# Keeping the split parts of a decoder's weights in DRAM between token quarters

## The chip, the cores and the metric

The kernel runs on one core of a Trainium2 chip. The metric is the device time of one execution in microseconds (us); lower is better. Three runs of the kernel before took 2722.57 to 2724.44 us, median 2723.67.

## The reference

One layer of a decoder trunk for 2048 tokens of 1024 channels, all in float32. Three groups of heads (GLA, HGRN2, mLSTM) mix the tokens chunk by chunk; one output projection and a squared-ReLU feed-forward follow. Cut to what matters here:

```python
h = modulated_rmsnorm(x, norm_mix[l], shift1, scale1)
z = h @ w_in[l]                       # 1024 -> 4,5k columns
mixed = concatenate([gla_group(...), hgrn2_group(...), mlstm_group(...)])
x = x + gate1 * (mixed @ w_out[l])    # 1024 x 1024
h = modulated_rmsnorm(x, norm_mlp[l], shift2, scale2)
x = x + gate2 * (square(relu(h @ w_ff1[l])) @ w_ff2[l])   # 1024 -> 4096 -> 1024
out = rms(x) * final_norm
```

## The kernel before, in words

The 2048 tokens are four quarters of 512 (`NQ`, `TQ`). First comes the input projection of all quarters (`inproj`), its results stored to DRAM. Then, quarter by quarter, the output projection (`outproj`) and the feed-forward, whose 32 hidden tiles go in six blocks (`f1` makes a hidden tile, `f2` adds a block's share to the accumulator `acc`). The token mixing (`block_pass`, `chunk`, `chunk_out`) is emitted in small steps between the dense products by `pump`, at a pace set by due times; the mixing of quarter q + 1 runs beside the feed-forward of quarter q and is done ahead of its last block, where `outproj` of quarter q + 1 stands too.

Dense products run in the format fp32r, which keeps fewer bits than float32. To hold float32's precision every operand is split in two parts, the rounded value (hi) and the rest (lo), and each product is three passes over the parts (`PASSES`). `split` (lines 175 to 177) makes them: a cast on ACT (L176) and a subtraction on DVE (L177).

Weights come in pieces of [128, 1024] float32, 512 KB. `weights` (line 179) loads a piece into a raw buffer (tag `raw`, two of them, SP's queue, L184) and splits it into a buffer `wt` of [128, 2, 1024], 1 MB (tag `wt`, three of them, four in the pool `lp` of the last quarter's last block). A quarter uses 8 pieces of w_out, 32 of w_ff1 and 32 of w_ff2, and every quarter loads and splits them anew: 288 loads. A piece serves 24 products of 128 x 512 (three passes of eight tiles).

A scheduler puts each engine's instructions in order when the program is built, by priorities that follow the order of the code, which `ahead()` raises by 60 instructions and `late()` lowers by 20, and by when buffers come free. On the chip each engine and each queue then works strictly in that order. SP's queue holds the weight loads, the stores of x1 (L930) and of the output (L1004), and the loads of x; POOL's queue holds the mixing's loads and stores and the loads of `acc`.

The last quarter's output projection is drawn ahead: it runs after the fourth block of the third quarter's feed-forward, with its operands in `lp`.

Of the kernel before, what the change touches and what calls it, by code (L numbers as in the profile page):

```python
# [6 lines left out]
F32 = mybir.dt.float32  # L7
F32R = mybir.dt.float32r
# [6 lines left out]
P = 128  # L15
# [5 lines left out]
EPS = 1e-6  # L21
# [80 lines left out]
def trunk(ctx, tc, I, out):  # L102
    nc = tc.nc
    V, A, G, T = nc.vector, nc.scalar, nc.gpsimd, nc.tensor
    dma = nc.sync.dma_start
# [44 lines left out]
    def ahead():  # L150
        """What the dense products wait for goes before the token mixing in each engine's order."""
        return tc.high_priority(offset=lead[0])
# [4 lines left out]
    def late():  # L157
        """Products of the token mixing give way to so many instructions that came after them."""
        return tc.high_priority(offset=-LATE)

# [8 lines left out]
    def ln_exp(after):  # L169
        """The set with Exp and Ln, behind the activation after; what the caller adds to the stack runs behind it."""  # L170
        with tc.issue_after(after.ins):
            p_ = A.preload_act_table_set("natural_log_exp_and_others")
        return tc.issue_after(p_.ins)
# [5 lines left out]
    def weights(src, n, lp=None):  # L179
        """A [128, n] piece of weights as its two parts, [128, 2, n]."""  # L180
        with ahead():
            raw = wp.tile([P, 1024], F32, tag="raw", name="raw", bufs=2)
            r = raw[:, 0:n]
            dma(out=r, in_=src)  # L184
            wt = (lp or wp).tile([P, 2, 1024], F32R, tag="wt", name="wt", bufs=4 if lp else 3)
            split(wt[:, 0, 0:n], wt[:, 1, 0:n], r)
        return wt[:, :, 0:n]
# [10 lines left out]
    def modulate(hi, lo, src, rs, a_, b_, tmp=None):  # L198
        """hi + lo = src * a_ * rs + b_; the product goes to src's place if there is no tmp."""
        tmp = src if tmp is None else tmp  # L200
        V.scalar_tensor_tensor(out=tmp, in0=src, scalar=a_, in1=rs, op0=ALU.mult, op1=ALU.mult)
        A.activation(out=hi, in_=tmp, func=AF.Identity, bias=b_)  # L202
        V.scalar_tensor_tensor(out=lo, in0=tmp, scalar=b_, in1=hi.bitcast(F32), op0=ALU.add, op1=ALU.subtract)

    def sq_acc(sm, src, first, over=False):
        """Adds src ** 2 (to be kept in src's place if over) and its share of EPS to sm."""
        if first:
            return A.activation(out=sm, in_=src, func=AF.Square)
        sq = src if over else m5()[:, 0:src.shape[-1]]
        last = A.activation(out=sq, in_=src, func=AF.Square)  # L210
        V.scalar_tensor_tensor(out=sm, in0=sm, scalar=EPS / 7 * KT, in1=sq, op0=ALU.add, op1=ALU.add)
        return last

    def newton(x, y, t, scale):
        """One step of y towards (x * scale + EPS) ** -0.5; x and t are overwritten."""
        V.tensor_scalar(out=x, in0=x, scalar1=scale, scalar2=EPS, op0=ALU.mult, op1=ALU.add)
        V.tensor_tensor(out=t, in0=y, in1=y, op=ALU.mult)
        V.scalar_tensor_tensor(out=t, in0=t, scalar=-0.5, in1=x, op0=ALU.mult, op1=ALU.mult)
        V.scalar_tensor_tensor(out=y, in0=t, scalar=1.5, in1=y, op0=ALU.add, op1=ALU.mult)
# [12 lines left out]
    # ---------------------------------------------------------------- conditioning  # L232
    ada_tags, acc_tags = [], ["prod", "sdt", "alb"]

    def ada(m, o, n, slow=False):
        """Channels o .. o + n of modulation vector m; slow: in steps and beside the rest, in the buffers of those."""
# [39 lines left out]
    # ---------------------------------------------------------------- token mixing  # L276
# [16 lines left out]
    def block_pass(q, s):  # L293
        """Scores of tokens at most 15 apart within blocks of 16 tokens, for 48 channels per group."""
# [27 lines left out]
    def gates(q):  # L322
        """mLSTM gate rows of a quarter (row 32 n + h: chunk n, head h): running stabiliser and what follows."""
# [77 lines left out]
    def chunk(q, n, L, N):  # L401
        """Up to the normalised outputs of chunk n; N is the next chunk of the quarter."""
        nxt = (lambda f: f(q, n + 1, N)) if N else (lambda f: None)
        pt = lambda nm: psm.tile([P, 512], F32, tag="psm", name=nm)
        # channel-major q, k, f
# [66 lines left out]
        # mLSTM scores  # L472
# [24 lines left out]
        # diagonal blocks of the gated groups' scores  # L497
# [9 lines left out]
        # mLSTM output  # L507
# [37 lines left out]
        # scores of the gated groups  # L545
# [71 lines left out]
        # norms, output gates  # L617
# [36 lines left out]
    def both(a, b):  # L654
        """The steps of two independent generators by turns."""
        its = [a, b]
        while its:
            for g in list(its):
                try:
                    yield next(g)  # L660
                except StopIteration:
                    its.remove(g)
# [14 lines left out]
    # ---------------------------------------------------------------- input projection  # L677
# [34 lines left out]
    def h_stats_slow(q, res):  # L712
        """The same for quarter q in steps, its loads a step ahead."""
        sm = stat("sm", 2)
        x = []
        for k in range(0, KT + 2, 2):
            x += [load_x(q, i) for i in range(k, min(k + 2, KT))]
            for i in range(max(k - 2, 0), k):
                last = sq_acc(sm, x[i], i == 0, True)
            yield  # L720
        rs = stat("rs", 1)
        rstd(rs, sm, last)
        res.append(rs)
# [6 lines left out]
    def inproj(q, hts, nxt):  # L730
# [62 lines left out]
        def part(g, c0, n, ps, kk):  # L793
            """Two k-tiles' share of n columns of a group (of n // 128 channel tiles of the convolution)."""
# [76 lines left out]
    # ---------------------------------------------------------------- output projection and feed-forward  # L871
    R.x1 = [dp.tile([P, KT, TQ], F32, name=f"x1{q}") for q in range(NQ)]

    def spare(spec, src):
        """Eight [128, 512] tiles in buffers that the chunks leave free, loaded from src."""
        ts = []
        for tag, n, bufs in spec:
            t = m1.tile([P, n, TQ], F32, tag=tag, name="spare", bufs=bufs)
            ts += [t[:, i, :] for i in range(n)]
        for k, t in enumerate(ts):  # L880
            dma_m(out=t, in_=src(k))
        return ts
# [23 lines left out]
    def outproj(q, mt, lp=None):  # L906
# [9 lines left out]
        for dt in range(KT):  # L916
            xr = xs[dt] if xs else load_x(q, dt)
            w = weights(I["wo"][dt].rearrange("p c n -> p (c n)"), 1024)
# [14 lines left out]
    def ffn_in(h2, q, xs, sm, last, lp=None):  # L933
        """The feed-forward's input into the list h2, in steps."""
# [16 lines left out]
    def f1(h2, ft):  # L951
        w = weights(I["w1"][ft].rearrange("p c n -> p (c n)"), 1024)
# [15 lines left out]
    def w2_part(b, i, lp=None):  # L968
        return weights(I["w2"][F0[b] + i].rearrange("p u n -> p (u n)"), 1024, lp)

    def f2_tile(hds, b, acc, w, dt, c):
        """Block b's share of channel tile dt for the tokens c of a quarter; w: from the number of a part to the part."""
# [33 lines left out]
    def final_steps(q, acc):  # L1006
        """The final norm of a quarter, in steps."""
        sm = stat("sm", 2)
        for dt in range(KT):
            last = sq_acc(sm, acc[:, dt, :], dt == 0)  # L1010
            if dt % 4 == 3:
                yield
        rs = stat("rs", 1)
        rstd(rs, sm, last)
        yield
        final(q, acc, rs)
        yield

    def f2_last(lp, hds, acc):
        """The last block and the final norm by halves of the tokens, the first norm beside the second half's products."""  # L1020
# [16 lines left out]
    # ---------------------------------------------------------------- schedule  # L1037
# [26 lines left out]
    def step():  # L1064
        """One step of the block passes (which run ahead) or of the chunks."""
# [10 lines left out]
    def pump(us):  # L1076
        """Token mixing beside us of dense products, at the pace that the nearest deadlines ask for."""
# [112 lines left out]
# How the emission of the token mixing is paced beside the dense products, in us of the tensor engine's dense work  # L1190
# where the comment gives no other unit.
SLACK = (20, 60, 60, 60)    # by which a quarter's mixing is to be done before it is due
LAST = 1480                 # when the last quarter's mixing is due
FILL = 20.0                 # mixing emitted behind the first quarter's output projection
LOAD = 5.0                  # from a block pass's loads to its arithmetic
RUN = 0.2                   # share of the next quarter's block passes that goes beside a quarter's chunks
AHEAD = 60                  # instructions by which weights and evacuations go before the mixing
LATE = 20                   # instructions by which the mixing's products give way
STATS = 14                  # step of the input projection at which the next quarter's norm starts
BG = (24, 12, 20)           # steps of the input projection beside which the other modulation vectors are made  # L1200
EARLY = 3                   # feed-forward block of the last but one quarter behind which the last one's x1 is made
# [19 lines left out]
```

## Time and profile before

| | us |
|---|---|
| median of three runs | 2723.67 |
| span of the profiled execution (first to last instruction) | 2721.9 |
| PE busy | 2636.9 (97%) |
| DVE busy | 1792.1 (66%) |
| ACT busy | 1231.6 (45%) |
| HBM read, written | 336.21 MB, 62.95 MB |

The profiled execution's own time is its span and what lies around it; the median of the runs is 1.8 us above that span. PE is TensorE's products, PEld its weight loads, DVE VectorE, ACT ScalarE, POOL GpSimd, SP the queue of SyncE. A row `ps_f<-ht,wt` names what an instruction writes and reads; `raw<-w` is a load of a feed-forward piece, `raw<-wo` one of w_out. "DMA share" is the mean busy share of the core's 16 DMA engines. Windows are in us from the start of the span.

By time: input projections to 842 us, output projection of the first quarter from 844, its feed-forward from 900, the second quarter's output projection from 1317, the third's from 1805, the fourth's from 2236, and dense products alone after that.

### The profile page before, as it was taken

How to read it: one execution, taken by the hardware profiler on the slowest of the kernel's cores; microseconds unless marked ns; L12 is line 12 of the kernel's file. 1: busy time of each engine (PE TensorE's matmuls, PEld its weight loads, DVE VectorE, ACT ScalarE, POOL GpSimd, SP SyncE). 2: the span in 40 equal slices, each digit the busy share in tenths (PEclk: the TensorE clock that was granted, in tenths of full speed). 3: DMA queues.
4: the chain of work that ended last, by engine and by line, in shares of the span. 5: the costliest groups of instructions: out<-in, count | busy, mean ns of one | idle time of the engine just before them, and what ended most of it. 6: DMA issues, size and time to landing. Idle time of an engine off the chain costs nothing.

```text
span 2721.9 us, 39555 instructions
## 1 busy us (share of the span) xinstructions
PE 2636.9 (97%) x15050; PEld 2212.7 (81%) x15050; DVE 1792.1 (66%) x3345; ACT 1231.6 (45%) x2190; POOL 259.2 (10%) x434
## 2 busy tenths in 40 slices
PE   6999999999999999999999999999999999999998
PEld 5888898898888777788877888788877788888887
DVE  8785687977776877776887655457556556533335
ACT  4654445445543543454453445345445543433333
POOL 0101110020201102112110000100000000000000
PEclk9999999999999999999999999999999999999999
DMA  8776675585547424445454333344433245342332
GB/s 259 222 227 185 176 238 167 174 231 176 160 140 217 116 82 135 126 133 165 132 177 125 118 120 113 117 140 146 145 119 111 89 129 176 107 146 93 95 99 78
DMA packets 160200, 401.76 MB, mean 148 GB/s; under 512 B 20473, under 2 KB 60490, under 8 KB 160010
## 3 DMA queue, kind: packets, MB, share of 16 engines
q1 hardware_dynamic: 129338, 306.51, 35.7%
q0 software_dynamic: 30672, 92.73, 12.4%
q8 instruction: 118, 1.93, 0.3%
q14 instruction: 72, 0.59, 0.1%
HBM read 336.21 MB, written 62.95 MB: 147 GB/s over the span
## 4 chain that ended last, share of the span: by engine, by line
PE 50%; DVE 2%; ACT 1%; DMA 1%; issue 0%; DVEq 0%; ACTq 0%; SPq 0%
PE ps_f L155 40%; PE ps_op L155 5%; PE ps_a L163 2%; DVE wt L177 1%; DMA raw<-w 1%; PE ps_oh L163 1%; PE ps_og L163 1%; PE ps_t L167 0%; PE ps_x L167 0%; DVE acc L1000 0%; PE ps_mv L163 0%; ACT wt L176 0%; PE ps_uh L163 0%; PE ps_ug L163 0%; PE ps_ms L155 0%
## 5 line engine op out<-in xcount | busy, mean ns | idle before, releaser
L155 PE MATMUL ps_f<-ht,wt 128*128 128x512 f32 (+1 forms) x5472 | 1307.9, 393 | 4.8 <-ACT ht L202 4.8
L155 PEld LDWEIGHTS ps_f<-ht,wt 128*128 128x128 f32 x5472 | 1003.9, 189 | 213.4 <-ACT ht L202 5.0
L177 DVE TENSOR_TENSOR wt<-raw,wt 128x1024 fp32r<-128x1024 f32 (+3 forms) x436 | 498.8, 1145 | 412.8 <-ACT wt L176 411.7
L176 ACT CAST wt<-raw 128x1024 fp32r<-128x1024 f32 (+3 forms) x436 | 431.4, 990 | 640.1 <-PE ps_f L155 345.3
L155 PE MATMUL ps_ip<-wt,ht 128*128 128x384 f32 (+2 forms) x3072 | 604.5, 353 | 32.9 <-ACT st L782 8.7
L155 PEld LDWEIGHTS ps_ip<-wt,ht 128*128 128x128 f32 x3072 | 550.4, 191 | 61.1 <-ACT st L782 10.3
L982 DVE SCALAR_TENSOR_TENSOR acc<-ps_f,mod,acc 128x512 f32<-128x512 f32 (+1 forms) x200 | 145.2, 727 | 129.2 <-PE ps_f L155 128.4
L962 ACT ACTIVATE m<-ps_f 128x512 f32<-128x512 f32 x128 | 76.7, 599 | 318.5 <-PE ps_f L155 318.2
L155 PE MATMUL ps_f<-h,wt 128*128 128x512 f32 x768 | 181.4, 397 | 0.0
L155 PEld LDWEIGHTS ps_f<-h,wt 128*128 128x128 f32 x768 | 144.6, 188 | 35.6 <-issue 0.5
L155 PE MATMUL ps_op<-ht,wt 128*128 128x512 f32 x576 | 133.1, 393 | 5.7 <-ACT ht L176 3.8
L155 PEld LDWEIGHTS ps_op<-ht,wt 128*128 128x128 f32 x576 | 108.8, 190 | 29.2 <-ACT ht L176 3.9
L301 POOL DMA_DIRECT2D blk<-zq x144 | 93.6, 663 | 344.1 <-DVE prod L311 204.2
L567 DVE TENSOR_TENSOR td<-ps_a,td 128x384 f32<-128x384 f32 (+2 forms) x96 | 40.6, 423 | 110.8 <-PE ps_a L163 110.3
L311 DVE TENSOR_TENSOR prod<-blk 128x768 f32<-128x768 f32 (+3 forms) x192 | 111.2, 579 | 2.9
L312 DVE TENSOR_REDUCE Sd<-prod 128x48 f32<-128x768 f32 (+3 forms) x192 | 110.5, 575 | 3.0
L965 DVE TENSOR_TENSOR ht<-m,ht 128x512 fp32r<-128x512 f32 x128 | 88.1, 688 | 22.8 <-ACT m L964 22.3
L310 DVE TENSOR_TENSOR blk<-blk 128x720 f32<-128x720 f32 (+4 forms) x180 | 98.9, 549 | 0.0
L155 PE MATMUL ps_ip<-ht,wt 128*128 128x512 f32 x384 | 98.4, 404 | 0.0
L155 PEld LDWEIGHTS ps_ip<-ht,wt 128*128 128x128 f32 x384 | 71.4, 191 | 14.9 <-issue 0.7
L964 ACT ACTIVATE m<-m 128x512 f32<-128x512 f32 x128 | 81.0, 633 | 2.6
L963 ACT ACTIVATE ht<-m 128x512 fp32r<-128x512 f32 x128 | 81.1, 634 | 0.1
(393 smaller groups left out, 2627.2 us busy)
## 6 DMA issues: line engine op xcount, KB each, us to landing
raw<-w SPq DMA_DIRECT2D x256, 512.0 KB, 3.5
raw<-wg SPq DMA_DIRECT2D x100, 384.0 KB, 3.8
m<-wada SPq DMA_DIRECT2D x64, 256.0 KB, 3.7
raw<-wo SPq DMA_DIRECT2D x32, 512.0 KB, 3.5
m<-xq SPq DMA_DIRECT2D x56, 256.0 KB, 3.3
raw<-wg SPq DMA_DIRECT2D x28, 512.0 KB, 4.4
blk<-zq POOLq DMA_DIRECT2D x144, 96.0 KB, 6.1
zt<-zq POOLq DMA_DIRECT2D x48, 288.0 KB, 3.9
```

The lines of the kernel that those rows point to most:

```text
L155: T.matmul(out=ps, lhsT=l, rhs=r, start=start, stop=stop)
L163: T.matmul(out=ps, lhsT=l, rhs=r, start=start, stop=stop)
L176: A.copy(out=hi, in_=src)
L177: V.tensor_tensor(out=lo, in0=src, in1=hi.bitcast(F32), op=ALU.subtract)
L301: dma_m(out=t[i][32 * g:32 * g + 32], in_=src)
L310: V.tensor_tensor(out=t[1][:, 0:n, :], in0=t[1][:, 0:n, :], in1=t[2][:, d:16, :], op=ALU.mult)
L311: V.tensor_tensor(out=prod[:, 0:n, :], in0=t[1][:, 0:n, :], in1=t[0][:, d:16, :], op=ALU.mult)
L312: V.tensor_reduce(out=s49[:, 0:n, d:d + 33:16], in_=prod[:, 0:n, :].rearrange("p j (u c) -> p j u c", c=16), op=ALU.add, axis=AX.X)
L963: A.activation(out=hd[:, 0], in_=r, func=AF.Square)
L964: A.activation(out=r, in_=r, func=AF.Square)
L965: V.tensor_tensor(out=hd[:, 1], in0=r, in1=hd[:, 0].bitcast(F32), op=ALU.subtract)
L982: V.scalar_tensor_tensor(out=acc[:, dt, c], in0=ps, scalar=mod[:, 40 + dt:41 + dt], in1=acc[:, dt, c], op0=ALU.mult, op1=ALU.add)
```

## The change

The first use of each piece of w_out, w_ff1 and w_ff2 stays a load and a split, and the two parts are then stored to a DRAM tile of their own (`kept`). Each later use of the same piece loads both parts, 1 MB, from there straight into `wt`, with no raw buffer and no split. The store of a piece is held back by one piece (`save(1)`: at most one stays unsaved when the next raw load is issued), and all that are left are stored ahead of a load from `kept` (`save(0)`). The keys are the matrix and the number of the piece. `weights` takes its `wt` buffer ahead of the raw buffer now. The pieces of the input projection have no key and are treated as before. The change also drops docstrings and comments, so line numbers shift by up to 17.

```diff
+    kept, unsaved = {}, []
+
+    def save(left):
+        while len(unsaved) > left:
+            dst, wt = unsaved.pop(0)
+            dma(out=dst, in_=wt.bitcast(F32))
+
-    def weights(src, n, lp=None):
+    def weights(src, n, lp=None, key=None):
         with ahead():
+            wt = (lp or wp).tile([P, 2, 1024], F32R, tag="wt", name="wt", bufs=4 if lp else 3)
+            if key in kept:
+                save(0)
+                dma(out=wt.bitcast(F32), in_=kept[key])
+                return wt
+            save(1 if key else 0)
             raw = wp.tile([P, 1024], F32, tag="raw", name="raw", bufs=2)
             r = raw[:, 0:n]
             dma(out=r, in_=src)
-            wt = (lp or wp).tile([P, 2, 1024], F32R, tag="wt", name="wt", bufs=4 if lp else 3)
             split(wt[:, 0, 0:n], wt[:, 1, 0:n], r)
+            if key:
+                kept[key] = dp.tile([P, 2, 1024], F32, name="parts_%s%d" % key)
+                unsaved.append((kept[key], wt))
         return wt[:, :, 0:n]
...
-            w = weights(I["wo"][dt].rearrange("p c n -> p (c n)"), 1024)
+            w = weights(I["wo"][dt].rearrange("p c n -> p (c n)"), 1024, None, ("o", dt))
...
-        w = weights(I["w1"][ft].rearrange("p c n -> p (c n)"), 1024)
+        w = weights(I["w1"][ft].rearrange("p c n -> p (c n)"), 1024, None, ("a", ft))
...
-        return weights(I["w2"][F0[b] + i].rearrange("p u n -> p (u n)"), 1024, lp)
+        return weights(I["w2"][F0[b] + i].rearrange("p u n -> p (u n)"), 1024, lp, ("b", F0[b] + i))
```

What that makes of the order, at three places. SP's queue at the passage from the first quarter's output projection to its feed-forward, before:

```order
L184 DMA raw<-wo 128x1024
L913 DMA acc<-xq 128x512 x8
L184 DMA raw<-wo 128x1024 x3
L184 DMA raw<-w 128x1024 x60
L184 DMA raw<-wo 128x1024 x5
```

and with the change (`parts_o` and `parts_a` are DRAM tiles of w_out and w_ff1; L185 is the store, L199 the raw load):

```order
L185 DMA parts_o_8198<-wt 128x2048
L199 DMA raw<-wo 128x1024
L185 DMA parts_o_8250<-wt 128x2048
L199 DMA raw<-w 128x1024
L185 DMA parts_o_8288<-wt 128x2048
L199 DMA raw<-w 128x1024
L185 DMA parts_a_8388<-wt 128x2048
L199 DMA raw<-w 128x1024
```

A store stands between each two loads of the first quarter: that of piece n ahead of the load of piece n + 2.

SP's queue at the passage from the second quarter's feed-forward to the third's, where the second quarter's output is stored, before:

```order
L930 DMA x_149<-spare 128x512
L184 DMA raw<-w 128x1024 x8
L1004 DMA out<-acc 128x1024 x4
L184 DMA raw<-w 128x1024 x43
L184 DMA raw<-wo 128x1024 x4
```

and with the change (`parts_a` and `parts_b` are the parts of w_ff1 and w_ff2; L194 is the load of parts, L1021 the store of the output):

```order
L194 DMA wt<-parts_a_8520 128x2048
L194 DMA wt<-parts_a_8567 128x2048
L194 DMA wt<-parts_a_8678 128x2048
L194 DMA wt<-parts_b_8744 128x2048
L1021 DMA out<-acc 128x1024 x4
L194 DMA wt<-parts_b_8788 128x2048
L194 DMA wt<-parts_b_8834 128x2048
```

The loads of parts take the places of the raw loads, and the stores of out move up by one load: seven loads of the new quarter stand ahead of them, where eight stood.

ACT's order at the start of the third quarter's output projection, before (`ht<-spare` is the cast of a mixed tile, `ht<-m` that of a hidden tile, `wt<-raw` that of a weight piece):

```order
L964 ACTIVATE m_16030<-m_16030 128x512
L962 ACTIVATE m_16069<-ps_f_16041 128x512
L176 CAST wt<-raw 128x1024
L963 ACTIVATE ht<-m_16069 128x512
L964 ACTIVATE m_16069<-m_16069 128x512
L962 ACTIVATE m_16108<-ps_f_16080 128x512
L176 CAST wt<-raw 128x1024
L963 ACTIVATE ht<-m_16108 128x512
L176 CAST ht<-spare 128x512
```

and with the change:

```order
L981 ACTIVATE m_15976<-m_15976 128x512
L979 ACTIVATE m_16012<-ps_f_15984 128x512
L980 ACTIVATE ht<-m_16012 128x512
L981 ACTIVATE m_16012<-m_16012 128x512
L979 ACTIVATE m_16048<-ps_f_16020 128x512
L980 ACTIVATE ht<-m_16048 128x512
L176 CAST ht<-spare 128x512
```

The casts of the weight pieces are gone, and the cast of the first mixed tile follows the hidden tile's directly.

## The prediction

> **What bounds the kernel now.** I read the page first, then the busy time by stretches of 100 us, the chain of waits in order of time, and the waits of PE alone.
>
> ```profile
> span 2721.9 us, 39555 instructions
> PE 2636.9 (97%) x15050; PEld 2212.7 (81%) x15050; DVE 1792.1 (66%) x3345; ACT 1231.6 (45%) x2190; POOL 259.2 (10%) x434
> ```
>
> PE is busy in 97% of the span, DVE in two thirds, ACT in under a half. The 85 us that PE lacks lie mostly ahead of the stages that the change touches, as the stretches show (columns: stretch, its length, busy us of PE, PEld, DVE, ACT and POOL, granted clock, DMA share, GB/s):
>
> ```profile
> 0.00:100.00 100.00, 69.93 (x333) 62.09 (x333) 86.73 (x192) 48.86 (x77) 4.17 (x14) 0.98 0.80 254
> 900.00:1000.00 100.00, 99.22 (x561) 78.98 (x561) 77.41 (x152) 42.48 (x67) 12.87 (x21) 0.95 0.34 93
> 1100.00:1200.00 100.00, 100.00 (x630) 80.07 (x629) 74.46 (x164) 51.89 (x110) 18.81 (x30) 1.00 0.49 144
> 1300.00:1400.00 100.00, 95.55 (x416) 78.24 (x415) 87.48 (x148) 50.13 (x78) 15.65 (x26) 0.98 0.49 144
> 1600.00:1700.00 100.00, 100.00 (x628) 80.88 (x627) 59.47 (x129) 49.26 (x105) 8.43 (x14) 1.00 0.41 130
> 2400.00:2500.00 100.00, 100.00 (x435) 81.55 (x434) 36.69 (x40) 33.11 (x44) 0.00 (x0) 1.00 0.30 95
> ```
>
> The first quarter's feed-forward runs from about 900 us, the last quarter's ends with the kernel. In these stretches PE has no time left to win but for single waits, and those are few. From 1300 us to the end, these are all of PE's waits (us in total, times, longest):
>
> ```profile
> PE ps_ms L155 <- DVE sm L211: 5.2, 3, 2.6
> PE ps_op L155 <- ACT ht L176: 3.8, 2, 1.9
> PE ps_mv L163 <- DVE alb L487: 1.2, 1, 1.2
> PE ps_x L167 <- DVE mx L638: 0.3, 1, 0.3
> ```
>
> They sum to 10.5 us. None is a wait for a weight piece. The chain of waits says the same of the pace: dense products follow one another in a fixed step, with mixing beside them or without.
>
> ```profile
> 1607.30 16.36 PE ps_f L155 x72
> 2370.58 315.46 PE ps_f L155 x1368
> ```
>
> The first row, taken where DVE is busy in 59% of the time, gives 16.36 / 72 = 227 ns a product, the second, where it is busy in some 37%, 315.46 / 1368 = 231 ns. Less work on DVE and ACT buys PE nothing here.
>
> **The change part by part.** First, the splits that go. Quarters two to four use 8 + 32 + 32 = 72 pieces each, 216 in all.
>
> ```profile
> L177 DVE TENSOR_TENSOR wt<-raw,wt 128x1024 fp32r<-128x1024 f32 x316 | 385.8, 1222 | 350.6 <-ACT wt L176 350.0
> L176 ACT CAST wt<-raw 128x1024 fp32r<-128x1024 f32 x316 | 332.1, 1051 | 506.3 <-PE ps_f L155 345.3 <-PE ps_op L155 58.7 <-PE ps_ip L155 37.9
> ```
>
> 216 x 1.222 = 264 us leave DVE and 216 x 1.051 = 227 us leave ACT. Nearly all of this lay beside PE's work. It was on the path in one kind of place, the start of an output projection, where the cast of a weight piece stands in ACT's order just ahead of the cast of the first mixed tile, for which PE waits:
>
> ```profile
> 1802.81 0.60 ACT L962 ACTIVATE m<-ps_f 128x512 f32<-128x512 f32 x1 [2.71 <-PE ps_f L155]
> 1803.31 1.04 ACT L176 CAST wt<-raw 128x1024 fp32r<-128x1024 f32 x1
> 1804.24 0.63 ACT L963 ACTIVATE ht<-m 128x512 fp32r<-128x512 f32 x1
> 1804.77 0.61 ACT L176 CAST ht<-spare 128x512 fp32r<-128x512 f32 x1
> 1805.43 4.90 PE L155 MATMUL ps_op<-ht,wt 128*128 128x512 f32 x20 [1.88 <-ACT ht L176]
> ```
>
> With the CAST of wt gone from ACT's order the mixed tile is cast 1.04 us sooner; what is late next is the cast of ht ahead of it, so 0.8 us of the 1.88 stay. There are two such starts (the row ps_op of PE's waits): -2.1 us. The waits of ps_ms hang on squares and sums that stay, one of them at the very end; I count nothing for them. The bound of all gain is the 10.5 us, less the last of the three ps_ms waits.
>
> Second, the 72 stores of 1 MB in the first quarter. They issue on SP, one after each 0.5 MB load, and wait for the split of their piece.
>
> ```profile
> SPq L184 <- DVE wt L177: 359.4, 58, 22.4
> ```
>
> That row (the first quarter, 860 to 1320 us) says that SP already waits there for splits 58 times, since a load needs a raw buffer that the split frees. A store of piece n stands ahead of load n + 2, which waits for the same split, so it holds nothing back that was free. A wt buffer now comes free when PE is done and the store has landed; the store issues about two pieces ahead of PE's use, so PE is the later. What remains is traffic. From 900 to 1315 us 60 pieces are used: 62.9 MB more in 415 us, 152 GB/s, on top of a mean of some 123 (93 in the stretch from 900, 144 in that from 1100). The sum, 275 GB/s, against the pace that the rows give for a share of one: 144 / 0.49 = 294, 95 / 0.30 = 317, 254 / 0.80 = 317. So it fits, at about nine tenths, with loads that land later. A weight load in the first quarter still has its two raw buffers and three wt buffers, some 19 us of lead, and PE waits for no mixing load in the trace. Cost: 0, with the bounds 0 and +34 us (below).
>
> Third, the loads of later quarters: 1 MB instead of 0.5, into wt itself. A load now waits for PE to be done with the piece three before it, and must land while PE works on the two between. A piece is 24 products: 24 x 0.2306 = 5.53 us, so 11.1 us are there, 10.9 at the faster step.
>
> ```profile
> raw<-w SPq DMA_DIRECT2D x256, 512.0 KB, 3.5
> DMA to landing us min/median/max: 2.9/3.5/9.3
> ```
>
> The second row is of the raw loads from 1330 to 2660 us. Half a megabyte more takes 0.524 MB / 317 GB/s = 1.7 us, so the median is 5.2 us (estimate from these rows), which leaves 5.7 of 10.9. In the steady state nothing shows. The longest landings come where the finished quarter is stored and the next accumulator is loaded:
>
> ```profile
> 1851.74 43.27 SPq L184 DMA_DIRECT2D raw<-w  x8
> 1896.73 4.91 SPq L1004 DMA_DIRECT2D out<-acc  x4
> 1902.48 10.73 SPq L184 DMA_DIRECT2D raw<-w  x3
> DMA to landing us min/median/max: 8.0/8.6/9.3
> ```
>
> (The last row: raw loads issued from 1890 to 1915 us.) There 9.3 + 1.7 = 11.0 meets the window of 10.9 to 11.1. SP's order moves too: the four stores of out stood behind eight loads of the new quarter and now stand behind seven. The eighth load then cannot issue ahead of out, which was ready at 1896.7 to 1901.6; but it needs the buffer of the fifth piece, and PE is through with that near 1902. The store costs it nothing. Three such places, 0 to 1.5 us each: I take +1.
>
> Fourth, what else moves. Stretches at the start of an output projection hold loads of spare tiles beside the weights; 1.7 us later for one at most, three times, covered by the tiles that are split meanwhile: +0.5. PE's order is all but the same, thirteen transposes of one chunk standing together where four and the rest apart stood: 0.
>
> Sum: -2.1 + 0 + 1 + 0.5 = -0.6 us on the span of 2721.9. The median of the runs, 2723.67, lies 1.8 above that span; the same 1.8 on top gives 2723.
>
> **The rivals.** One: the bursts stall PE (slower). The mechanism is the one of the third part: a three-buffer lead, with SP issuing only when PE is done. The price decides from 11.0 us of landing on. If the whole landing of a burst doubled with its bytes, 2 x 8.6 = 17.2, a stall would be 6.2 us, and three places give 19; between that and 0 I put +8: 2731. For it: the burst row. Against: two loads in the row were in flight together, and now one is. The Trainium skill (DMA: Bandwidth & Descriptors, section Bandwidth) has 6.15 us of transfer for 1 MB against the 3.3 that 317 GB/s gives; by that the median would still land in time, and a burst load 2.8 us too late, 8.4 us in all. No run here shows a 1 MB load alone.
>
> Two: the first quarter becomes bound by DMA (slower). If the 254 GB/s of the first stretch is the most that lasts, 275 x 415 / 254 = 449 us are needed where 415 are: +34, 2757. Against it: a share of 0.80 in that stretch, and this one:
>
> ```profile
> 1890.00:1920.00 30.00, 30.00 (x133) 24.79 (x133) 19.07 (x25) 13.37 (x20) 2.12 (x4) 1.00 0.69 245
> ```
>
> 245 GB/s at 0.69 is a pace of 355.
>
> Three: the relief of DVE and ACT takes all waits that it can (faster): 10.5 - 2.3 of the last norm = 8.2 us, and with the wait near 1364 us the half-speed clock behind it (0.98 in the stretch from 1300, 2 us lost at most): -10, 2714. For it: those waits do hang on ACT and DVE. Against: their chains keep all their own steps. The Trainium skill (Perfetto Trace Analysis, section Identifying the Most-Contended Engine) calls busy matmuls a bad measure and asks for the share of LDWEIGHTS, here 81%; by that PE would have a fifth in hand, and the gain could be larger. The trace disagrees: 227 to 231 ns a product whatever the other engines do.
>
> That pieces are split again after all is excluded by the order: none of the 216 splits is left in it.
>
> **How the numbers follow.** Forecast 0.56, bursts 0.21, first quarter 0.08, relief 0.15. A measurement of this kernel tells about 0.2%, 5.4 us, from no change: 2718.2 to 2729.1 is "same". So faster 0.15, same 0.56, slower 0.21 + 0.08 = 0.29. The likeliest case alone has 2719 to 2728. The range reaches to the relief, 2713, and to the upper half of the bursts, 2738; it leaves out the first quarter's 0.08 and the tails of the two others.
>
> **What would show it.** In the profile after: DVE near 1792 - 264 = 1528 us and ACT near 1005; HBM reads up by 113 MB and writes by 75; a dense step of 227 to 231 ns still; ps_op's wait of 1.9 near 0.8. I am wrong if PE waits for wt from a DMA in more than single places (then, at the out stores or all through the dense quarter?), if the first quarter, 900 to 1315 us, is longer by more than 3 us, or if PE's waits fall by more than 5.

## The result, and the profile after

The changed kernel is slower: 2737.96 us median of 6 runs (2733.65 to 2748.33) beside 2724.06 us for the kernel before (2721.72 to 2732.18, 6 runs), a ratio of 1.0051 with a 95% interval of 1.0034 to 1.0069. The same kernel measured again gave 1.0047 (1.0029 to 1.0065).

The page of the profiled execution (span, busy time, traffic) first.

```profile
span 2731.9 us, 39036 instructions
PE 2641.2 (97%) x15050; PEld 2214.8 (81%) x15050; DVE 1544.4 (57%) x3129; ACT 1029.0 (38%) x1974; POOL 260.0 (10%) x434
HBM read 449.45 MB, written 138.45 MB: 215 GB/s over the span
```

The change did what it says. DVE has lost 248 us, ACT 203 us; 113 MB more are read and 75 MB more written. The dense step is the old one: the chain of waits has the same 1368 products in the same time as before.

```profile
2380.46 315.46 PE ps_f L155 x1368
```

The span has grown by 10.0 us all the same. All waits of PE from 995 us on, changed kernel:

```profile
PE ps_ms L155 <- DVE sm L228: 5.3, 3, 2.6
PE ps_x L167 <- DVE mx L655: 4.1, 3, 3.5
PE ps_op L155 <- DVE ht L177: 2.7, 1, 2.7
PE ps_op L155 <- ACT ht L176: 2.2, 2, 1.1
PE ps_op L155 <- DMA wt<-parts_o: 1.6, 1, 1.6
PE ps_mv L163 <- DVE alb L504: 1.4, 1, 1.4
PE ps_f L155 <- DMA wt<-parts_b: 0.2, 1, 0.2
```

For weights that come by DMA PE waits 1.8 us in all. New are a wait for DVE's part of a mixed tile (ht, 2.7), a longer one for mx (ps_x, 3.5), and one for alb near 1202 us (1.4; the kernel before has its one of 1.2 near 1463).

To see where the time went, each of the 10464 dense products is set against the same product of the kernel before. For nine stretches (in us by the clock of the kernel before), the table has how much longer it is from the start of a stretch's first product to the start of its last than in the kernel before. For 1314 to 1330 and for 2060 to 2085 two parts of the growth are added in brackets: that of PE's idle time, and that of the time lost to a granted clock of 0.5 while PE was not idle. The rows below the first are profiled executions of the experiments, one for each.

| us | 844-995 | -1200 | -1214 | -1314 | -1330 | -1480 | -2060 | -2085 | -2690 | sum |
|---|---|---|---|---|---|---|---|---|---|---|
| changed kernel | +1.0 | 0.0 | +1.7 | +0.4 | +6.6 (3.6, 2.6) | -3.4 | -1.3 | +5.0 (3.5, 1.7) | +1.2 | +11.1 |
| the same again | -1.0 | 0.0 | +1.7 | +0.5 | +5.8 (2.8, 2.6) | -4.1 | -1.3 | +3.3 (3.3, 0) | +0.6 | +5.5 |
| stores only | -0.6 | 0.0 | +3.7 | +1.5 | +7.2 (3.7, 3.4) | +4.0 | +1.4 | 0.0 | 0.0 | +17.3 |
| no stores | -0.7 | 0.0 | 0.0 | 0.0 | -0.6 | -5.3 | -1.2 | +3.8 (2.2, 1.7) | +0.5 | -3.6 |
| copy put back | +2.2 | 0.0 | +3.7 | +1.4 | +5.8 (3.4, 2.0) | -1.4 | -1.3 | +0.3 | +1.6 | +12.3 |
| nine stores only | +1.4 | 0.0 | 0.0 | +1.6 | +4.8 (2.7, 2.1) | -3.0 | 0.0 | 0.0 | 0.0 | +4.9 |
| all but the nine | -0.6 | 0.0 | +5.7 | 0.0 | -0.7 | -3.1 | -1.1 | +2.2 (2.2, 0) | +0.6 | +3.0 |
| half the bytes | -0.5 | 0.0 | 0.0 | 0.0 | -0.6 | -0.1 | -1.3 | +0.8 | +0.1 | -1.5 |
| nine from a constant | +0.9 | 0.0 | 0.0 | +0.1 | +5.9 (3.7, 2.0) | -2.6 | 0.0 | 0.0 | 0.0 | +4.2 |
| 36 early stores | +1.4 | 0.0 | 0.0 | 0.0 | -0.6 | -5.6 | -0.8 | 0.0 | 0.0 | -5.6 |
| w_out only | -2.8 | 0.0 | +1.2 | -0.2 | -0.6 | -3.2 | -0.9 | 0.0 | 0.0 | -6.5 |

Two places carry the loss: the second output projection (1314 to 1330) and one wait at 2067. A third, at 1200 to 1214, is smaller here. The -3.4 ahead of 1480 is for the most part no merit of the change: the two kernels with nine stores, whose engines run the order of before, have -3.0 and -2.6 there as well.

**The second output projection.** PE in the changed kernel (start, length, and in brackets the idle time ahead):

```profile
1318.74 0.74 PE L155 MATMUL ps_op<-ht,wt 128*128 128x512 f32 x2 [1.13 <-ACT ht L176]
1321.10 0.73 PE L155 MATMUL ps_op<-ht,wt 128*128 128x512 f32 x2 [1.63 <-DMA wt<-parts_o]
1324.58 5.63 PE L155 MATMUL ps_op<-ht,wt 128*128 128x512 f32 x13 [2.75 <-DVE ht L177]
```

Three waits stand where one of 1.88 us stood. The longest is for DVE's part of the first mixed tile. DVE's first product of the block pass, the split of a weight piece just ahead of it, and that mixed tile, before:

```profile
1289.22 1.22 DVE L177 TENSOR_TENSOR wt<-raw,wt 128x1024 fp32r<-128x1024 f32 x1
1290.35 0.95 DVE L311 TENSOR_TENSOR prod<-blk 128x768 f32<-128x768 f32 x1
1317.88 0.68 DVE L177 TENSOR_TENSOR ht<-spare,ht 128x512 fp32r<-128x512 f32 x1
```

and with the change:

```profile
1297.67 1.22 DVE L177 TENSOR_TENSOR wt<-raw,wt 128x1024 fp32r<-128x1024 f32 x1 [1.41 <-ACT wt L176]
1298.82 0.95 DVE L328 TENSOR_TENSOR prod<-blk 128x768 f32<-128x768 f32 x1
1323.84 0.69 DVE L177 TENSOR_TENSOR ht<-spare,ht 128x512 fp32r<-128x512 f32 x1
```

From that product to the mixed tile DVE needs less (25.0 us, before 27.5), but it starts 8.5 us later. It does not wait for blk there: the last blk has landed at 1292.8 us (before 1279.3), 6 us ahead, and in the whole trace DVE waits 0.4 us for it. What is late is the split ahead of the product, by the same 8.5 us. DVE waits for ACT's cast of the piece, and ACT for the load into the raw buffer (waits of ACT from 1255 to 1300 us, and two of the casts):

```profile
ACT wt L176 <- DMA raw<-w: 21.4, 5, 6.0
1271.43 1.05 ACT L176 CAST wt<-raw 128x1024 fp32r<-128x1024 f32 x1 [3.34 <-DMA raw<-w]
1285.75 1.05 ACT L176 CAST wt<-raw 128x1024 fp32r<-128x1024 f32 x1 [5.95 <-DMA raw<-w]
```

The kernel before has no such wait there. Its loads and stores issued from 1250 to 1295 us, with their median to landing:

```profile
DMA packets 2923, 9.12 MB, mean 203 GB/s; under 512 B 576, under 2 KB 832, under 8 KB 2921
q0 software_dynamic: 1712, 4.72, 41.3%
q1 hardware_dynamic: 1209, 4.36, 32.4%
raw<-w SPq DMA_DIRECT2D x8, 512.0 KB, 6.5
```

and with the change:

```profile
DMA packets 3687, 15.55 MB, mean 345 GB/s; under 512 B 650, under 2 KB 906, under 8 KB 2805
q1 hardware_dynamic: 1973, 10.79, 66.2%
q0 software_dynamic: 1712, 4.72, 33.6%
raw<-w SPq DMA_DIRECT2D x6, 512.0 KB, 11.5
```

In these 45 us the two queues held the 16 DMA engines for 41.3 + 32.4 = 74% of the time before, and for 66.2 + 33.6 = 99.8% with the stores. A raw buffer is loaded again only when its piece has been split. With 11.5 us for the load, 1.05 for the cast and 1.23 for the split, one of the two buffers is taken for some 14 us (an estimate, the sum of these), which is 7 us a piece. In the trace the five splits up to 1297.67 come 6.8 us apart, where the kernel before has 5.4, the pace of PE. PE has three wt buffers in hand and waits for none of these pieces. But DVE works in its order, so its share of the mixing stands behind the late splits, and the mixed tile behind that.

The waits cost more than their length. The stretches of 6 us around them (columns as in the prediction; the third number from the end is the granted clock):

```profile
1317.00:1323.00 6.00, 2.07 (x11) 1.11 (x9) 5.90 (x12) 5.98 (x13) 0.00 (x0) 0.99 0.72 298
1323.00:1329.00 6.00, 4.42 (x10) 3.47 (x11) 6.00 (x13) 1.98 (x4) 0.00 (x0) 0.50 0.00 0
1329.00:1335.00 6.00, 6.00 (x26) 4.94 (x25) 3.67 (x8) 2.79 (x8) 0.57 (x1) 0.94 0.50 116
```

The clock records of the trace have 0.5 for 6.83 us, from 1322.93 us on. PE is still idle for 1.65 us of these, and loses half of the rest, 2.6 us, on top of the 3.6 us of longer waits.

**The wait at 2067.** Before, ACT casts the parts of mx first and copies vaug from v later:

```profile
2060.88 1.33 ACT L632 ACTIVATE mx<-ps_oh,st 128x64 f32<-128x64 f32 x6
2066.21 0.49 ACT L489 COPY vaug<-v 128x256 f32<-128x256 f32 x1
```

With the change that copy stands ahead of them and waits for a load, and PE waits for mx behind it:

```profile
2067.22 0.41 ACT L506 COPY vaug<-v 128x256 f32<-128x256 f32 x1 [3.57 <-DMA v<-zv]
2067.53 1.33 ACT L649 ACTIVATE mx<-ps_oh,st 128x64 f32<-128x64 f32 x6
2073.22 0.63 PE L167 MATMUL ps_x<-cst,mx 128*128 128x128 f32 x4 [3.49 <-DVE mx L655]
```

Two casts of weight pieces that stood ahead of the copy are gone from ACT's order there, and the scheduler has moved the copy up into their room. The load of v lands in 7.5 us, beside loads of parts, where it took 3.8.

### The profile page after: what moved, and what is told of

Its sections match the earlier page's. It is cut to its first block, busy times and chain, and to the rows that moved or that the text cites. A ratio compares the mean times of both kernels' runs of the same rounds, so it can differ in the third digit from the quotient of the medians.

```text
span 2731.9 us, 39036 instructions
## 1 busy us (share of the span) xinstructions
PE 2641.2 (97%) x15050; PEld 2214.8 (81%) x15050; DVE 1544.4 (57%) x3129; ACT 1029.0 (38%) x1974; POOL 260.0 (10%) x434
## 3 DMA queue, kind: packets, MB, share of 16 engines
q0 software_dynamic: 30672, 92.73, 11.5%
## 4 chain that ended last, share of the span: by engine, by line
PE 48%; DMA 3%; DVE 2%; ACT 1%; issue 0%; SPq 0%; DVEq 0%; ACTq 0%
PE ps_f L155 39%; PE ps_op L155 4%; PE ps_a L163 2%; DMA raw<-w 1%; DMA m<-xq 1%; PE ps_oh L163 1%; PE ps_og L163 1%; PE ps_t L167 0%; PE ps_x L167 0%; DMA wt<-parts_b 0%; DMA v<-zv 0%; DVE wt L177 0%; PE ps_mv L163 0%; PE ps_qk L163 0%; ACT wt L176 0%
## 5 line engine op out<-in xcount | busy, mean ns | idle before, releaser
L177 DVE TENSOR_TENSOR wt<-raw,wt 128x768 fp32r<-128x768 f32 (+3 forms) x220 | 235.0, 1069 | 182.4 <-ACT wt L176 181.6
L176 ACT CAST wt<-raw 128x768 fp32r<-128x768 f32 (+3 forms) x220 | 204.4, 929 | 331.1 <-PE ps_ip L155 127.3
L228 DVE SCALAR_TENSOR_TENSOR sm<-sm,m 128x512 f32<-128x512 f32 (+1 forms) x91 | 58.9, 647 | 42.8 <-ACT m L227 41.6
```

The source lines that it names most:

```text
L176: A.copy(out=hi, in_=src)
L177: V.tensor_tensor(out=lo, in0=src, in1=hi.bitcast(F32), op=ALU.subtract)
```

## The experiments

Two theories were set against each other. **Stores**: the 72 stores share the DMA engines with the mixing's loads, which land late, and PE stands where it needs what DVE makes of them. **Order**: the room that the splits leave lets the scheduler put mixing steps ahead of what PE waits for (on DVE at 1320 us too, where four more rows of the block pass stand ahead of the mixed tile). The stores theory was put with the mixing's loads as what is late. At 1320 it is the weight loads, as shown above; whether the stores make the stall is tested all the same. Ratios are to the kernel before, timed beside each.

### The changed kernel again

> The changed kernel once more, beside the other three, so that each is set against it in the same runs. Every theory expects a ratio of 1.003 to 1.007 to the kernel before. The theories of the +10 us in the profiled span. Stores theory: the 72 stores of the first quarter delay the mixing's loads (blk and spare land in 7 to 14 us instead of 5 to 8), so DVE is late with the block pass, and PE stands at the start of the second output projection; that is +3.5 us near 850 to 900 us and +7 near 1320. Order theory: with the splits gone, the scheduler puts steps of the mixing ahead of what PE waits for, on DVE near 1320 us and on ACT near 2067 us. Both theories expect PE's waits at those places here again.

1.0047 (1.0029 to 1.0065). The waits at 1320 (3.0 us for DVE's ht) and 2067 (3.3 us for mx) are there again.

### The stores without their use

```diff
-            if key in kept:
-                save(0)
-                dma(out=wt.bitcast(F32), in_=kept[key])
-                return wt
-            save(1 if key else 0)
+            save(1 if key and key not in kept else 0)
...
-            if key:
+            if key and key not in kept:
```

> The stores of the first quarter as in the changed kernel, but the later quarters load raw pieces and split them as before; nothing reads the stored parts. DVE's order at the second output projection is that of the kernel before. Stores theory: blk lands near 1293 us instead of 1279, DVE needs 27.5 us from its first product to the first mixed tile as before, so that tile comes near 1326 instead of 1318, and PE stands 6 us or more there: +8 to +13 us in all, ratio 1.003 to 1.005; no wait of ps_x near 2069. Order theory: no stall at 1320, within 2 us of the kernel before, ratio 0.999 to 1.001.

2744.29 us, 1.0079 (1.0061 to 1.0097): worse than the change itself. The waits of PE that have grown, from 900 us on:

```profile
PE ps_ms L155 <- DVE sm L224: 7.4, 3, 4.8
PE ps_mv L163 <- DVE alb L500: 3.3, 2, 1.9
PE ps_op L155 <- DVE ht L177: 3.2, 1, 3.2
PE ps_kt L167 <- ACT X L427: 1.9, 1, 1.9
```

The stall at 1320 is there (+7.2 us) with DVE's old order, and ps_x has no such wait at 2067. So the stores make the one, and not the other. They cost more than was expected: in this trace the gain of the later quarters is missing, and a wait of 4.8 us for ps_ms comes on top.

### The use without the stores

```diff
-                kept[key] = dp.tile([P, 2, 1024], F32, name="parts_%s%d" % key)
-                unsaved.append((kept[key], wt))
+                one = [v for k, v in kept.items() if k[0] == key[0]]
+                kept[key] = one[0] if one else dp.tile([P, 2, 1024], F32, name="parts_%s%d" % key)
+                if not one:
+                    unsaved.append((kept[key], wt))
```

> The orders of the changed kernel on PE, and but for some rows on DVE and ACT, without its stores: of each matrix only the first piece is stored (3 stores instead of 72), and every later load of 1 MB reads the parts of that one piece, so the products of quarters two to four use wrong weights. Stores theory: blk lands near 1279 us again, the first mixed tile of the second output projection near 1315, no stall there, and none of the +3.5 us before 900; what stays is the wait of ps_x near 2065 (+4), less 2 us of gain at the output projections: 0 to +4 us, ratio 1.000 to 1.0015. Order theory: the stall of DVE's order at 1320 stays, +8 to +10 us, ratio 1.003 to 1.004. A third theory, that the 1 MB loads by themselves cost, gives waits of ps_f or ps_op for wt from a DMA, more than 3 us in sum.

2726.47 us, 1.0007 (0.9993 to 1.0021). All waits of PE from 995 us on:

```profile
PE ps_ms L155 <- DVE sm L230: 3.4, 2, 2.7
PE ps_x L167 <- DVE mx L657: 2.8, 3, 2.2
PE ps_op L155 <- ACT ht L176: 2.2, 2, 1.1
```

Nothing at 1200 or 1320, though DVE has the order of the changed kernel there: the order theory falls for that place. The wait for mx at 2060 stays, as the stores theory had it. No wait for a weight load is left, so the 1 MB loads by themselves, here of the same three DRAM tiles over and over, cost PE nothing.

### One copy of ACT put back

```diff
+    R.mx_last = None
...
+        with tc.issue_after(R.mx_last.ins) if q == NQ - 1 and n else ExitStack():
-        A.copy(out=vaug[:, :, 0:64], in_=L.v[:, 768:1024].rearrange("p (h c) -> p h c", c=64))
+            A.copy(out=vaug[:, :, 0:64], in_=L.v[:, 768:1024].rearrange("p (h c) -> p h c", c=64))
...
-            A.activation(out=mx[:, 64 * h:64 * h + 64], in_=pog[:, 64 * h:64 * h + 64], func=AF.Copy,
+            R.mx_last = A.activation(out=mx[:, 64 * h:64 * h + 64], in_=pog[:, 64 * h:64 * h + 64], func=AF.Copy,
```

> The changed kernel with one copy of ACT (vaug from v, which waits for the load of v) put back behind the last quarter's mx activations, where it stood before the change; a single instruction moves by eight rows of ACT's order. Order theory for the place near 2069 us: ACT no longer stands 3.6 us for that load ahead of mx, PE's wait of 3.5 us for mx goes, and the span is 3.5 to 4.3 us shorter than the changed kernel's: ratio to the kernel before 1.0035 where the changed kernel has 1.005. Rival: what is late there is the load of v itself (7.5 us to landing instead of 3.8), and the wait moves on to the next reader of vaug: no gain, ratio as the changed kernel's.

In the trace the order theory holds for this place: ACT goes on to mx after a wait of 0.69 us for DVE, and the stretch from 2060 to 2085 costs 0.3 us where the changed kernel has 5.0 and 3.3.

```profile
2072.17 1.34 ACT L651 ACTIVATE mx<-ps_oh,st 128x64 f32<-128x64 f32 x6 [0.69 <-DVE st L236]
```

The ratio is 1.0051 (1.0032 to 1.0069), not the 1.0035 expected. Its interval is 10 us wide, so 3.5 us neither show nor are excluded by it; in the profiled execution the wait at 1205 us happened to be worse (+3.7 instead of +1.7) and took 2 us of it.

### Nine stores alone, and all but these nine

The nine lie beside the mixing's burst of loads. In the first kernel of the two they are the only edit to the kernel before; in the second they are left out of the change.

The first, as an edit to the kernel with the stores without their use:

```diff
+    HELD = [("a", f) for f in range(25, 29)] + [("b", f) for f in range(23, 28)]
...
-            if key and key not in kept:
+            if key in HELD and key not in kept:
```

The second, as an edit to the change, with the same list:

```diff
-            if key:
+            if key and key not in HELD:
```

> The kernel before, with nine of the stores added and nothing else: those of the pieces 25 to 28 of w_ff1 and 23 to 27 of w_ff2, which lie beside the mixing's burst of loads from 1250 to 1290 us. Nothing reads what they store, and the orders of PE, DVE, ACT and POOL are those of the kernel before, row for row. Theory of the place (stores beside the burst delay blk, DVE's block pass and the first mixed tile): nothing until 1250 us, then blk lands 6 to 13 us later than 1279, the first mixed tile comes at 1324 to 1328, and PE loses 5 to 8 us at the start of the second output projection; ratio 1.002 to 1.003. Rival, that the loss comes from the stores as a whole, in many places: under 3 us, ratio below 1.001.

> The changed kernel without these nine stores; their nine pieces are split again in each quarter. Theory of the place: blk lands by 1283 us, no stall over 2 us at the second output projection, 5 to 7 us less than the changed kernel: ratio 1.002 to 1.003. Rival, the stores as a whole: 63 of 72 stores stay, and so do seven eighths of the loss, ratio 1.0045.

Nine alone: 1.0014 (0.9999 to 1.0030), with +4.8 us at the second output projection. The same steps as in the changed kernel are there: 340 GB/s from 1250 to 1295 us with 11.8 us for a raw load, the split ahead of the block pass late, then the mixed tile, with PE waiting for it (in order of time),

```profile
1294.69 1.23 DVE L177 TENSOR_TENSOR wt<-raw,wt 128x1024 fp32r<-128x1024 f32 x1 [0.97 <-ACT wt L176]
1320.62 0.68 DVE L177 TENSOR_TENSOR ht<-spare,ht 128x512 fp32r<-128x512 f32 x1
1321.36 3.87 PE L155 MATMUL ps_op<-ht,wt 128*128 128x512 f32 x10 [2.68 <-DVE ht L177]
```

and the clock at half (a stretch of 6 us):

```profile
1317.00:1323.00 6.00, 3.32 (x8) 2.17 (x9) 5.93 (x13) 5.55 (x10) 0.00 (x0) 0.53 0.37 119
```

The half clock sets in at 1317.38 us, ahead of this wait: it follows PE's wait of 1.88 us for ACT's ht, which the kernel before has too, there without it. So a part of these 4.8 us is chance.

All but the nine: 1.0017 (1.0007 to 1.0027), no stall there (-0.7 us), a third of the changed kernel's loss where the rival had seven eighths. What I had not expected is +5.7 us at 1200 to 1214. There other stores delay a load of the mixing, sdt (8.0 us to landing, before 5.1). DVE waits for it, and PE for what DVE makes later, alb:

```profile
1195.18 0.84 DVE L517 TENSOR_REDUCE dsum<-sdt 128x96 f32<-128x384 f32 x1 [1.77 <-DMA sdt<-sd]
1203.93 1.84 PE L163 MATMUL ps_mv<-vaug,alb 128*128 128x65 f32 x8 [2.22 <-DVE alb L505]
```

PE's wait is 2.2 us, and a clock of 0.5 for 6.83 us behind it makes up the rest. So the place theory is right on its place and too narrow: a second burst, at 1165 to 1215, is hit by other stores.

### Half the bytes, and bytes that wait for no split

The first is an edit to the change, the second one to the kernel with nine stores alone:

```diff
-            dma(out=dst, in_=wt.bitcast(F32))
+            dma(out=dst, in_=wt[:, 0, :].bitcast(F32))
...
-                dma(out=wt.bitcast(F32), in_=kept[key])
+                for p in range(2):
+                    dma(out=wt[:, p, :].bitcast(F32), in_=kept[key])
...
-                kept[key] = dp.tile([P, 2, 1024], F32, name="parts_%s%d" % key)
+                kept[key] = dp.tile([P, 1024], F32, name="parts_%s%d" % key)
```

```diff
-            dma(out=dst, in_=wt.bitcast(F32))
+            with tc.issue_after(R.raw.ins):
+                for i in range(4):
+                    dma(out=dst[:, i // 2, 512 * (i % 2):512 * (i % 2) + 512], in_=cst[:, 0:512])
...
-            dma(out=r, in_=src)
+            R.raw = dma(out=r, in_=src)
```

> The changed kernel with stores of half the bytes: only the rounded part of each piece is stored, 0.5 MB, and later quarters load it twice, so the lower parts are left out of the products of quarters two to four. Traffic theory (what delays the mixing's loads is the bytes that share the DMA engines): blk lands about half as late, near 1286 us, the stall at 1320 is 0 to 3 us, ratio 1.001 to 1.003. Queue theory (a store that waits for its split stands ahead of a raw load in SP's queue, or holds its wt buffer): the count and the order of the stores are the same, so the loss stays, ratio 1.0045 or more.

> As the kernel with nine stores alone, but each store takes its 1 MB, in four DMAs, from a constant that lies in SBUF from the start, so it waits for no split and holds no wt buffer; the orders of PE, DVE, ACT and POOL are those of the kernel before. Traffic theory: the same loss as from the nine stores of wt, 5 to 8 us at the second output projection, ratio 1.002 to 1.003. Queue theory: none, ratio 0.999 to 1.001.

These two set the bytes against the queueing. Half the bytes, with as many stores at the same places of SP's queue: 1.0010 (0.9996 to 1.0024), nothing at 1200 and at 1320 (its loads of weights come in two DMAs each, and PE waits 3.5 us for them in two later places). Its traffic and raw loads, issued from 1250 to 1295 us:

```profile
DMA packets 4143, 13.66 MB, mean 304 GB/s; under 512 B 688, under 2 KB 944, under 8 KB 4140
raw<-w SPq DMA_DIRECT2D x9, 512.0 KB, 6.1
```

Nine stores from a constant, which wait for no split and hold no buffer, in an order that is otherwise that of before: +5.9 us at the second output projection, as from the nine of wt, with the same wait of PE:

```profile
PE ps_op L155 <- DVE ht L177: 3.4, 1, 3.4
```

The ratio, 1.0010 (0.9995 to 1.0024), is too wide to tell 6 us from none; the trace is what speaks. The queue theory as it was put, a wait for the split or a held buffer, falls on both: with these kept and the bytes halved the stall goes, with the bytes kept and these gone it stays. But the second kernel does not free SP's queue. From 1255 to 1300 us its raw loads wait 3.6 + 2.7 + 0.4 = 6.7 us for earlier DMAs to land, where SP in the changed kernel waits for splits alone. And no run tells two ways apart in which the bytes can delay a raw load: by sharing the engines with all queues, or as the store of 1 MB that goes ahead of it in SP's queue. In the changed kernel such a load lands 1.2 to 3.4 us behind that store.

### Versions without the stores that hurt

```diff
+    EARLY_W = [("o", i) for i in range(8)] + [("a", i) for i in range(17)] + [("b", i) for i in range(11)]
...
-            if key:
+            if key in EARLY_W:
```

The second kernel has the eight pieces ("o", i) alone in that list.

> The changed kernel with the first 36 pieces of the first quarter kept (w_out, 17 of w_ff1, 11 of w_ff2, used up to about 1100 us) and the others split anew in each quarter, so no store stands beside the mixing's loads from 1170 to 1290 us. ACT's copy of v stands behind mx again in this order, as before the change. Theory (stores beside the mixing's loads at 1200 and 1320 us, and that copy at 2067 us, are the whole loss): none of the three waits is there, the shorter waits at the output projections stay (0 to -5 us from 1310 to 1860), so 2 to 5 us less than the kernel before: ratio 0.998 to 0.9995. Rival (the loads of 1 MB, or a store anywhere, cost as well): ratio 1.001 or more, with waits of PE elsewhere.

> The changed kernel with the eight pieces of w_out alone kept, all 64 feed-forward pieces split anew in each quarter. Theory of the prediction's first term: PE's waits of 1.9 us for ht at the starts of the second and third output projections fall to 1.1 us each, nothing else moves: 2 us less than the kernel before, ratio 0.999 to 1.000. Rival: a new order of DVE or ACT brings a wait of its own, ratio 1.001 or more.

With 36 early stores: 2720.97 us, 0.9991 (0.9977 to 1.0005), span 2715.7. All of PE's waits from 900 us on:

```profile
PE ps_f L155 <- ACT ht L220: 3.4, 1, 3.4
PE ps_ms L155 <- DVE sm L229: 3.1, 3, 2.3
PE ps_op L155 <- ACT ht L176: 2.2, 2, 1.1
PE ps_x L167 <- DVE mx L656: 0.6, 2, 0.3
```

The three waits are gone, and this version is faster than the changed kernel (0.9991 beside 1.0047 and 1.0051, each to the kernel before, with intervals that do not meet). That it is faster than the kernel before cannot be told from no change. W_out alone: 1.0005 (0.9991 to 1.0019). The waits for ht at the two starts are 1.1 us each as expected, but the waits for alb are 2.9 us in two places where the kernel before has 1.2 in one, so a new order brought a little of its own, as the rival had it.

## Why the prediction was wrong

It said no change at 2723 us, with a range to 2738. The median came out at that edge, 2738, and clear of the kernel before. The range reached so far for the sake of a rival that did not occur (stalls at the stores of out), so that the time lies at its edge is luck.

- **First, the splits that go (-2.1).** Right in the mechanism, a little too large. PE's wait for ht at the starts fell from 3.8 to 2.2 us, so -1.6, and what was late next was the cast ahead of it, as said; 1.1 us stayed at each start instead of 0.8. At the second start the stall swallowed the gain.
- **Second, the stores ("Cost: 0").** This step failed. It held the mean of 415 us against the pace of the engines (275 of 294 to 317 GB/s), and as a mean that fits: from 900 to 1300 us the changed kernel moves 267 GB/s, and from 995 to 1200 us the change costs 0.0. But the mixing's loads come in bursts. In the 45 us from 1250 the engines were held for 74% of the time already, and the stores filled them. A raw load then took 11.5 us instead of 6.5. The step gave the weights "some 19 us of lead", and for PE that was enough. It did not ask what a late load does to DVE, which splits the pieces: DVE's order puts the block pass and the mixed tile behind the splits, and PE waits for that tile. "PE waits for no mixing load in the trace" is true and beside the point too: at 1200 us DVE waits for one (sdt), and PE for DVE. In place of 0 the runs have 6.6 us at 1320 and 1.7 at 1200, up to 5.7 there in other runs.
- **Third, the loads of 1 MB (+1).** Right. They land in 4.9 to 5.0 us where 5.2 were estimated; PE waits 0.2 us for a feed-forward piece, and 1.6 us once for one of w_out, inside the stall at 1320. In both profiles PE waits for no weights at the stores of out, which speaks against the first rival.
- **Fourth, what else moves (+0.5).** PE's order was indeed all but the same. Late loads at the starts, for which the +0.5 stood, are the 1.6 us just named (0.6 in the second profile). The other failure is that only PE's order was weighed for what moved: one copy of ACT went ahead of mx and cost 3.3 to 5.0 us in a stretch that cost 0.3 with the copy behind.
- **The rivals.** The second had the right resource and the wrong mechanism: the first quarter as a whole is not bound by DMA. Its signal, 900 to 1315 us longer by 3 us, didn't come, since the harm shows only at 1318, where the tile is due. The third, the relief, shows in traces at most: where no store stands in the way, the sum is -3.6 (no stores) and -5.6 us (36 early stores), but some 3 of these lie where kernels without any relief have them too, and both ratios (1.0007, 0.9991) cannot be told from 1.

The two profiled executions of the changed kernel show +11.1 and +5.5 us, the medians +13.9 and +12.1. Each of the two was the fastest run of its six. What the other runs lost beyond these is not located; the runs of one kernel scatter by some 15 us, and a clock that answers the same wait at one time and not at another (below) may be part of that.

## What to carry to other kernels

Set added traffic against the busiest tens of microseconds that it will overlap, not against the mean, and ask which engine waits for those loads and what stands behind in its order. A lead in buffers protects the engine that reads them, not the one that fills them. Where work is taken off an engine with a fixed order, compare that engine's own order at the places where the bound engine waits for it: a scheduler fills the room, also with an instruction that waits for a load. A path through DVE or ACT that ends just in time is part of the bound even if no wait for it shows yet.

## What the runs showed of the hardware

The granted clock goes to 0.5 in periods of 3.41 us or two or three of them (the clock records of the traces: 3413, 6827, 10240 ns; the last one of each trace ends with it). Within each of the twelve traces these records start and end on one grid of 3413 ns, to 5 ns. It is not the length of a wait of PE that decides whether the half clock follows, but how much of one period of the grid PE idles. Of the periods at full clock from 844 to 2690 us, in all twelve traces, those with 1.96 us or more of waits were all followed by one at half clock (24 of 24), those with 1.42 to 1.92 us in 11 cases of 21, and those with less in none, but for three near 972 to 982 us in which PE did not wait and ran mostly the mixing's small products. So the wait of 3.32 us near 2068 (the changed kernel again) set off nothing, with 1.41 and 1.92 us in two periods, and that of 3.49 us in the first profile did, with 2.76 us in one. Where the grid lies differs from trace to trace, so the same wait counts at one time and not at another. The Trainium skill (TensorE: Matmul & The Clock Gate, section What's actually happening) has the activity watched in free-running windows of 3413 ns. These records agree. In the places given here the half clock cost 1.7 to 3.4 us on top of the wait.

At some 340 GB/s with the engines held all the time, a 512 KB load of w took 11.5 us to land instead of 6.5, a 96 KB load of blk 9.2 instead of 6.7; at 304 GB/s w took 6.1 and blk 6.8 (medians of the loads issued from 1250 to 1295 us). So an eighth less traffic gave back the delay; the stores ahead of the loads of w were half as long there, too.
